# Two-layer hybrid encoder on one core: the second norm's sum moved into the middle of the second FFN pair, and three attention-projection tiles built together

## The chip, the cores and the metric

One core of a Trainium2 chip. A core has a matrix engine (TensorE, PE in the profile; its weight loads are listed apart as PEld), three engines for the rest (VectorE = DVE, ScalarE = ACT, GpSimd = POOL), and queues that issue transfers (SP = SyncE, and POOL). The metric is the device time of one execution in microseconds (us). Before the change it is 1625.27 us, the median of three runs (1622.42 to 1626.29).

## The reference

Two layers over 512 positions of 1024 channels. Each layer has three parallel branches (differential attention, a Conformer convolution, a Fourier mixing), which are gated, merged and projected, and then a SwiGLU FFN with its own RMSNorm. The change touches the attention branch's last projection and the FFN:

```python
gates = jax.nn.sigmoid(h @ w_gate[l] + b_gate[l]).reshape(b, s, N_BRANCH, d)
merged = gates[:, :, 0] * y_a + gates[:, :, 1] * y_b + gates[:, :, 2] * y_c   # y_a = att @ w_proj_a
x = x + merged @ w_out[l]

h2 = rmsnorm(x, norm2_g[l])
f_gate, f_up = jnp.split(h2 @ w_ffn_in[l], 2, axis=-1)
x = x + (jax.nn.silu(f_gate) * f_up) @ w_ffn_out[l]
```

`rmsnorm(x, g)` is `x * rsqrt(mean(x*x) + EPS) * g`, with one scale for each position. The hidden width of the FFN is 2816, which is 22 tiles of 128.

## The kernel before, in words

**Layout.** Activations lie transposed: a tile is 128 channels by 512 positions. Each operand of a matmul is split in a high part in a reduced format and a low part, the rest; a product is three matmuls (high x high, low x high, high x low). Weights come as chunks of 128x1024 by DMA and are split on chip: ScalarE casts the high part, and VectorE subtracts (L210, L317), or ScalarE negates and a transfer issued by POOL adds the weights on top (L309, L331).

**Order.** The kernel gives each instruction a priority, `self.t`, a running clock of TensorE work; `self.at(t)` sets it. A scheduler, which runs when the program is built, sorts the instructions of all engines by these priorities and by its own model of what is ready. Each engine then takes its own list strictly from the front. The lists differ from the code's order, so the sections below show rows of these lists.

**Attention projection.** `main` first builds the attention outputs `self.atts`, four pairs of tiles (high, low); the last one becomes ready last. `gemm_two` (L237) takes two output tiles m=0 and 1 and runs the first three of four steps for both, then the last step for both. `gemm` (L223) runs the other six tiles one by one.

**The FFN's first half.** After the output projection, `combine` makes the operands of Strassen's scheme with half-size blocks. `pair_gemm` (L370) computes gate and up of one hidden tile (a pair) with seven block products in two PSUM banks, `b1` and `b2`. Four of the products come first (`first`, 12 matmuls each: a11, s1, s3, s2, 48 matmuls of 128x256). Then `p15` keeps a sum of the two banks (a copy on ScalarE, L389, and an addition on VectorE, L390), and three more products (a12, s4, a22; 36 matmuls) go into the same banks. Pairs use the banks in turn: tag "s" for pair 0, "att" for pair 1, "main" for pair 2, and "s" again for pair 3. So the first matmul of pair 3 must wait until `unit` of pair 0 has read both "s" banks.

**The second norm.** The weights are applied to x before it is normalised, and the scale `rb2` is multiplied in afterwards, in `unit` (L605: L608 to L617). `sq_add` collects the squares of x as the output projection makes them (a square on ScalarE, L411, and an addition on POOL, L416). `inv_rms` (L419) adds them over channels with one matmul against a matrix of ones (tile `oth`, float32), then makes 1/sqrt by a table function on ScalarE (L428) and one Newton step: L426 and L431, L432 on VectorE, L430 on ScalarE. With its last argument `True` the ones matmul is ordered behind the last matmul issued so far (`self.after`). It is called after the whole of pair 1 (L633, L634), and the units of pairs 0 and 1 follow.

**Rounds.** Hidden tiles are taken in rounds of 6, 6, 6 and 4; after each round the round's part of the second FFN matrix is multiplied (L642). All 48 first matmuls of a pair need its split weights: tiles `whi`, `wlo`, and the sums s1, s2, s4 in `qst`/`kst` for even pairs, `A` for odd ones. Halves of the weights of odd pairs come into `cv` tiles; VectorE's first sum of a pair (L310) waits for these transfers.

Of the kernel before, what the change touches and what calls it, by code (L numbers as in the profile page):

```python
# [18 lines left out]
D = 1024  # L19
T = 512  # L20
NT = T // P
KT = D // P
# [35 lines left out]
LAG_N = 5000  # L58
LAG_S = 20000
LAST = (2500, 8000)  # L60
LN = (6000, 14000, 29000)
PEORD = False
CONV_LOW = -20000
# [30 lines left out]
class Hybrid:  # L94
# [139 lines left out]
        self.at(self.t)  # L234
        return ps

    def gemm_two(self, xs):  # L237
        banks = [self.bank(), self.bank()]
        n = len(xs)
        ws = [[self.wtile() for _ in xs] for _ in banks]  # L240
        for ks in (range(n - 1), (n - 1,)):
            for ps, w in zip(banks, ws):
                for k in ks:
                    wh, wl = w[k]
                    xh, xl = xs[k]
                    self.at(self.t)
                    self.mm(ps, wh, xh, k == 0, False)
                    self.mm(ps, wh, xl, False, False)
                    self.lastmm = self.mm(ps, wl, xh, False, k == n - 1)
                    self.t += 3 * PASS  # L250
                    self.poll()
        self.at(self.t)
        return banks
# [113 lines left out]
                out[n] = (hi[:, s], lo[:, s])  # L367
        return out

    def pair_gemm(self, u, w, xc, split_k=False):  # L370
        nc = self.nc
        tag = ("s", "att", "main")[u % 3]
        b1, b2 = self.bank(tag), self.bank(tag)
        h = T // 2
        n = len(xc)

        def x(name):
            return [p[name] for p in xc]

        first = (  # L380
            (b1[:, 0:h], "a11", "b11", True), (b1[:, h:T], "s1", "t1", False),
            (b2[:, h:T], "s3", "t3", True), (b2[:, 0:h], "s2", "t2", False),
        )
        steps = (list(range(n - 1)), [n - 1]) if split_k else (list(range(n)),)
        for ks in steps:
            for i, (ps, a, b, start) in enumerate(first):
                self.product(ps, w[a], x(b), ks, start and ks[0] == 0, i % 2 == 1 and ks[-1] == n - 1)
        p15 = self.slot("M")
        nc.scalar.copy(p15, b1)  # L389
        nc.vector.tensor_tensor(out=p15, in0=b2, in1=p15, op=ALU.add)  # L390
        ks = list(range(n))
        self.product(b1[:, 0:h], w["a12"], x("b21"), ks, False, False)
        self.product(b1[:, h:T], w["s4"], x("b22"), ks, False, True)
        self.product(b2[:, h:T], w["a22"], x("t4"), ks, False, True)
        return b1, b2, p15
# [153 lines left out]
    def main(self, l):  # L549
        nc = self.nc  # L550
        self.by_dma = False
        self.glu(l)
        if l == 0:
            self.tables()
        self.qkv(l)
        self.heads(l, self.t + ATT0, ATT)
        self.by_dma = True
        self.four_c(l)
        merged = self.merged
        ths = []  # L560
        for m in range(KT):
            pg = self.gemm(self.h)
            ths.append(self.tanh(pg, 0, m, "A"))
        thb = [self.tanh(self.gemm(self.h), 1, m, "M") for m in range(LEAD_B)]
        self.drain("conv")
        for m in range(KT):
            py = self.gemm(self.cvs)
            self.merge(m, thb.pop(0), py)
            if m + LEAD_B < KT:
                thb.append(self.tanh(self.gemm(self.h), 1, m + LEAD_B, "M"))  # L570
        self.drain("att")
        ms = []

        def merge_a(m, py):
            self.merge(m, ths[m], py)
            ms.append(self.split_to(merged[m], "cv" if m < 4 else "A"))

        for m, py in enumerate(self.gemm_two(self.atts)):
            merge_a(m, py)
        for m in range(2, KT):  # L580
            merge_a(m, self.gemm(self.atts))
        self.by_dma = False
        x2, xc, acc = [None] * KT, [], None
        g2 = self.par(l, "g2")
        h = T // 2
        for q in range(KT // 2):
            us = self.wtp.tile([P, 2, T], F32, tag="wth", name=self.nm("us"))
            ts = self.wtp.tile([P, 2, T], F32, tag="wtl", name=self.nm("ts"))
            for i, m in enumerate((q, q + KT // 2)):
                xr = self.slot("M")  # L590
                self.at(self.t - 20000)
                getattr(nc, QS[3]).dma_start(xr, self.xin[m])
                self.at(self.t)
                ps = self.gemm(ms)
                xt = self.slot("V")
                nc.vector.scalar_tensor_tensor(out=xt, in0=ps, scalar=0.5, in1=xr, op0=ALU.mult, op1=ALU.add)
                nc.scalar.activation(us[:, i, :], xt, AF.Copy, scale=g2[:, m : m + 1])
                acc = self.sq_add(xt, acc, "M")
                x2[m] = xt
            xc.append(self.combine(us[:, 0, :], us[:, 1, :], (ts[:, 0, :], ts[:, 1, :]), XCT[q]))  # L600
        self.xg, self.acc = [], None
        xin = []
        rb2 = None

        def unit(j, b1, b2, qw, scaled):  # L605
            z = self.slot("M")
            v = nc.vector.tensor_tensor
            v(out=z[:, 0:h], in0=b1[:, 0:h], in1=rb2[:, 0:h], op=ALU.mult)  # L608
            v(out=z[:, h:T], in0=b1[:, h:T], in1=qw[:, 0:h], op=ALU.add)
            v(out=z[:, h:T], in0=z[:, h:T], in1=rb2[:, h:T], op=ALU.mult)  # L610
            nc.scalar.activation(z, z, AF.Silu)
            u = self.slot("M")
            v(out=u[:, 0:h], in0=b2[:, h:T], in1=qw[:, 0:h], op=ALU.add)
            v(out=u[:, h:T], in0=qw[:, 0:h], in1=qw[:, h:T], op=ALU.add)
            if scaled:
                v(out=u, in0=u, in1=rb2, op=ALU.mult)
            v(out=u, in0=u, in1=z, op=ALU.mult)  # L617
            if j < 4:
                t = self.wtp.tile([P, 2, T], F32R, tag="wth" if j < 2 else "wtl", name=self.nm("act"))
                return self.split(u, t[:, 0, :], t[:, 1, :])  # L620
            return self.split_to(u, "att")

        done = 0
        for rnd, nj in enumerate(ROUNDS):
            act = []
            held = []
            scaled = done + nj == NJ
            for j in range(nj):
                w = self.pair_weights(done + j)
                held.append((j, *self.pair_gemm(done + j, w, xc, done + j == 0), scaled))  # L630
                if done + j == 0:
                    continue
                if done + j == 1:  # L633
                    rb2 = self.inv_rms(acc, D, "ar", "rb", True)  # L634
                while held:
                    act.append(unit(*held.pop(0)))
            done += nj
            for m in range(KT):
                if scaled and l == L - 1 and m == KT - 1:
                    self.last_tile(m, act, x2[m])  # L640
                    continue
                y = ps = self.gemm(act)  # L642
                if not scaled:
                    y = self.slot("M")
                    nc.vector.tensor_tensor(out=y, in0=ps, in1=rb2, op=ALU.mult)  # L645
                nc.vector.tensor_tensor(out=x2[m], in0=y, in1=x2[m], op=ALU.add)
                if done < NJ:
                    continue
                if l == L - 1:
                    nc.sync.dma_start(self.out[m], x2[m])  # L650
                else:
                    sc = self.dram.tile([P, T], F32, tag=f"x{l}_{m}", name=f"x{l}_{m}")
                    getattr(nc, QS[3]).dma_start(sc, x2[m])
                    xin.append(sc)
                    self.next_x(l + 1, m, x2[m])
        self.xin = xin
        self.x = x2
# [208 lines left out]
    def heads(self, l, t0, span):  # L866
# [45 lines left out]
        def norm(hp):  # L912
            fs[hp] = self.head_cols(atts[hp], zs.pop(hp))
            self.t += 860
# [5 lines left out]
        for u in range(NH * NT):  # L920
# [7 lines left out]
            if u % 8 == 7:  # L928
                dn, ds = (LAG_N, LAG_S) if u < NH * NT - 1 else LAST
                self.later(t + LAG_T + LAG_V + dn, "att", lambda hp=u // 8: norm(hp))  # L930
# [166 lines left out]
    def conv(self, l, t0, span):  # L1097
# [82 lines left out]
        def up(fn):  # L1180
            self.at(self.tc.cur_priority - LN_UP)
            fn()

        t1 = t0 + span + PAUSE[1]
        for fn, dt in zip((ln0, ln1, ln2), LN):
            self.later(t1 + dt, "conv", lambda fn=fn: up(fn))
# [136 lines left out]
```

## Time and profile before

| what | value |
|---|---|
| median of 3 runs | 1625.27 us (1622.42 to 1626.29) |
| profiled execution, its own time | 1623.3 us |
| its span, first to last instruction | 1621.5 us |
| TensorE busy | 1593.5 us, 98% of the span |
| VectorE, ScalarE, POOL busy | 1309.1, 870.6, 183.6 us |
| mean granted TensorE clock | 0.993 of full speed |

The time is that of the execution, and the span leaves out 1.8 us around the instructions. A matmul's busy time is modelled and overlaps that of the next, so the distance between the starts of two matmuls is the better measure: 0.12 us for a 128x256 matmul of the FFN pairs at full clock. A view of waits names for each engine what it sat idle for, and a view by time lists instructions with their start, duration, and in square brackets the idle time before them and what ended it.

### The profile page before, as it was taken

What the parts mean: (1) busy time and instruction counts of PE and PEld (TensorE: products, weight loads), DVE (VectorE), ACT (ScalarE), POOL (GpSimd) and SP (SyncE); (2) the same over time, 40 slices, a digit from 0 to 9 for tenths busy, and PEclk for the clock granted to TensorE, in tenths of its full rate; (3) what the DMA queues carried; (4) which work ended last, traced back from release to release, by engine and by line L of the source; (5) the groups of instructions that cost most, each with busy time, mean ns of one, the idle gap of its engine ahead of it and who ended that gap; (6) DMA issues with size and microseconds to landing.
All of it is one profiled execution on the core that took longest, in us unless ns stands there. A gap on an engine that the chain in (4) does not pass through costs nothing.

```text
span 1621.5 us, 24447 instructions
## 1 busy us (share of the span) xinstructions
PE 1593.5 (98%) x9104; PEld 1395.3 (86%) x9104; DVE 1309.1 (81%) x2388; ACT 870.6 (54%) x1419; POOL 183.6 (11%) x162
## 2 busy tenths in 40 slices
PE   9999999999998999999999999999999899999999
PEld 7888888787888898999888888887878898989998
DVE  6999999775887786858779999996758878878684
ACT  6546556873565463535444565577635644546351
POOL 1000010113230000000100000020232300000000
PEclk9999999999999999999999999999999999999999
DMA  6556366455463554647432664554445535546361
GB/s 220 169 165 197 83 163 150 112 127 124 150 168 79 156 131 124 150 111 186 127 117 80 196 180 118 137 147 111 119 116 162 144 92 151 136 130 157 87 161 65
DMA packets 80471, 222.85 MB, mean 137 GB/s; under 512 B 11216, under 2 KB 12368, under 8 KB 80352
## 3 DMA queue, kind: packets, MB, share of 16 engines
q1 hardware_dynamic: 67392, 175.59, 34.5%
q0 software_dynamic: 12528, 45.17, 16.2%
q8 instruction: 72, 1.18, 0.3%
q10 hardware_dynamic: 432, 0.53, 0.1%
q14 instruction: 47, 0.39, 0.1%
HBM read 207.35 MB, written 13.89 MB: 136 GB/s over the span
## 4 chain that ended last, share of the span: by engine, by line
PE 92%; DVE 3%; DMA 2%; ACT 1%; issue 1%; SPq 0%; DVEq 0%; ACTq 0%
PE main L126 54%; PE s L342 10%; PE att L342 8%; PE main L342 8%; PE s L126 4%; PE att L126 3%; PE oth L126 3%; PE att L136 2%; DMA cv<-in_w 1%; DMA wr<-in_w 0%; PE att L835 0%; DVE wl L210 0%; DVE A L160 0%; DMA V<-in_xT 0%; DMA kst<-dqk 0%
## 5 line engine op out<-in xcount | busy, mean ns | idle before, releaser
L208 ACT CAST wh<-wr 128x1024 fp32r<-128x1024 f32 x178 | 186.2, 1050 | 244.2 <-PE main L126 130.5
L126 PE MATMUL main<-X,wh 128*128 128x512 f32 x864 | 278.6, 395 | 0.0
L210 DVE TENSOR_TENSOR wl<-wr,wh 128x1024 fp32r<-128x1024 f32 x138 | 176.6, 1280 | 37.6 <-ACT wh L208 37.0
L126 PEld LDWEIGHTS main<-X,wh 128*128 128x128 f32 x864 | 161.0, 189 | 32.5 <-issue 0.3
L1120 DVE SCALAR_TENSOR_TENSOR cv<-cv,hcw,cv 128x497 f32<-128x497 f32 (+14 forms) x240 | 180.4, 752 | 0.9
L126 PE MATMUL main<-X,wl 128*128 128x512 f32 x432 | 169.9, 393 | 0.0
L126 PE MATMUL main<-act,wh 128*128 128x512 f32 (+1 forms) x520 | 161.9, 391 | 0.0
L944 ACT ACTIVATE at<-s,mx 128x512 f32<-128x512 f32 x128 | 87.9, 688 | 59.0 <-DVE mx L942 50.2
L126 PEld LDWEIGHTS main<-act,wh 128*128 128x128 f32 x520 | 96.3, 188 | 21.7 <-DVE M L645 0.6
L126 PE MATMUL main<-A,wh 128*128 128x512 f32 x320 | 107.7, 393 | 0.0
L309 POOL DMA_DIRECT2D wlo<-in_w x44 | 37.8, 859 | 577.7 <-ACT wlo L308 172.9
L126 PE MATMUL main<-att,wh 128*128 128x512 f32 x320 | 100.0, 393 | 3.0 <-ACT att L159 3.0
L942 DVE TENSOR_REDUCE mx<-s 128x1 f32<-128x512 f32 x128 | 86.6, 683 | 19.3 <-PE s L126 18.7
L126 PE MATMUL main<-act,wl 128*128 128x512 f32 (+1 forms) x260 | 101.4, 391 | 0.0
L126 PE MATMUL main<-wh,X 128*128 128x512 f32 x288 | 96.7, 392 | 0.0
L126 PEld LDWEIGHTS main<-X,wl 128*128 128x128 f32 x432 | 81.5, 189 | 16.5
L331 POOL DMA_DIRECT2D wl<-in_w x40 | 34.5, 864 | 518.9 <-ACT wl L330 357.2
L126 PE MATMUL main<-cv,wh 128*128 128x512 f32 x240 | 76.8, 392 | 0.0
L126 PEld LDWEIGHTS main<-att,wh 128*128 128x128 f32 x320 | 59.7, 188 | 17.4 <-ACT att L159 3.5
L126 PE MATMUL main<-A,wl 128*128 128x512 f32 x192 | 74.4, 390 | 0.0
L126 PEld LDWEIGHTS main<-A,wh 128*128 128x128 f32 x320 | 59.7, 188 | 11.9
L126 PEld LDWEIGHTS main<-wh,X 128*128 128x128 f32 x288 | 53.8, 188 | 11.1
(371 smaller groups left out, 4206.7 us busy)
## 6 DMA issues: line engine op xcount, KB each, us to landing
wr<-in_w SPq DMA_DIRECT2D x222, 512.0 KB, 3.8
wlo<-in_w POOLq DMA_DIRECT2D x44, 512.0 KB, 5.6
wl<-in_w POOLq DMA_DIRECT2D x40, 512.0 KB, 7.6
cv<-in_w SPq DMA_DIRECT2D x80, 256.0 KB, 4.7
dqk<-at SPq DMA_DIRECT2D x32, 256.0 KB, 4.6
qst<-dqk SPq DMA_DIRECT2D x96, 64.0 KB, 2.2
kst<-dqk SPq DMA_DIRECT2D x96, 64.0 KB, 2.0
V<-in_xT SPq DMA_DIRECT2D x8, 256.0 KB, 7.1
```

Source lines behind the costliest of these rows:

```text
L126: return self.pin(self.nc.tensor.matmul(out, lhsT=lhsT, rhs=rhs, start=start, stop=stop))
L136: self.pin(self.nc.tensor.transpose(ps[:, s], src[:, s], self.ident))
L208: nc.scalar.copy(hi, raw)
L210: nc.vector.tensor_tensor(out=lo, in0=raw, in1=hi.bitcast(F32), op=ALU.subtract)
L309: nc.gpsimd.dma_start(l2, src2, accum_op=ALU.add)
L331: self.nc.gpsimd.dma_start(lo, src, accum_op=ALU.add)
L342: self.nc.tensor.matmul(ps, lhsT=a[:, s], rhs=b, start=start and k == ks[0] and i == 0, stop=last and i == 2, skip_group_check=True,)
L942: nc.vector.tensor_reduce(out=mx, in_=ps, axis=AX.X, op=ALU.max, negate=True)
L944: nc.scalar.activation(e, ps, AF.Exp, bias=mx, accum_out=z1 if c else z0)
L1120: ins = nc.vector.scalar_tensor_tensor(out=acc[:, a:b], in0=g[:, a + d : b + d], scalar=w[:, t : t + 1], in1=acc[:, a:b], op0=ALU.mult, op ...
```

## The change

Two parts.

1. `gemm_two` becomes `gemm_few(xs, few)` and is called with 3: three attention-projection tiles run their first three steps, and then their last.
2. `pair_gemm` gets an argument `mid`, a function that it calls between the four first products and the `p15` copy. For pair 1 that function is `norm`, which calls `inv_rms` with a priority 15000 earlier than the running clock. So the ones matmul is tied to the last matmul of pair 1's first four products, where it was tied to the last matmul of the pair, and all instructions of `inv_rms` get an earlier priority.

```diff
+EARLY = 15000
...
-    def gemm_two(self, xs):
-        banks = [self.bank(), self.bank()]
+    def gemm_few(self, xs, few):
+        banks = [self.bank() for _ in range(few)]
...
-    def pair_gemm(self, u, w, xc, split_k=False):
+    def pair_gemm(self, u, w, xc, split_k=False, mid=None):
...
                 self.product(ps, w[a], x(b), ks, start and ks[0] == 0, i % 2 == 1 and ks[-1] == n - 1)
+        if mid is not None:
+            mid()
         p15 = self.slot("M")
...
-        for m, py in enumerate(self.gemm_two(self.atts)):
+        for m, py in enumerate(self.gemm_few(self.atts, 3)):
             merge_a(m, py)
-        for m in range(2, KT):
+        for m in range(3, KT):
             merge_a(m, self.gemm(self.atts))
...
+        def norm():
+            nonlocal rb2
+            self.at(self.t - EARLY)
+            rb2 = self.inv_rms(acc, D, "ar", "rb", True)
+            self.at(self.t)
+
...
-                held.append((j, *self.pair_gemm(done + j, w, xc, done + j == 0), scaled))
+                held.append((j, *self.pair_gemm(done + j, w, xc, done + j == 0, norm if done + j == 1 else None), scaled))
                 if done + j == 0:
                     continue
-                if done + j == 1:
-                    rb2 = self.inv_rms(acc, D, "ar", "rb", True)
                 while held:
```

No instruction is added or removed. Line numbers below 60 stay, later ones grow by 1 to 9 (L342 becomes L343, L426 becomes L429, L608 becomes L617). How the lists of the engines change is shown at three places, all in the first layer; the second layer has the same moves.

**TensorE in the FFN's first round, before.** `att` are the banks of pair 1, `main` those of pair 2, `oth` the ones matmul.

```order
L342 MATMUL att_4883<-B_4719,whi_4855 128x256
L342 MATMUL att_4883<-B_4720,whi_4855 128x256
L342 MATMUL att_4883<-B_4719,wlo_4856 128x256
L126 MATMUL oth_4971<-M_4701,ones 128x512
L342 MATMUL main_5036<-at_4411,whi_5011 128x256 x2
```

The same engine with the change; `s` are the banks of pair 0.

```order
L343 MATMUL att_4883<-B_4715,A_4871 128x256
L343 MATMUL att_4883<-B_4716,A_4871 128x256
L343 MATMUL att_4883<-B_4715,A_4872 128x256
L127 MATMUL oth_4932<-M_4701,ones 128x512
L343 MATMUL s_4754<-X_4414,whi_4731 128x256
```

The ones matmul stood behind the last product of pair 1; it now stands behind pair 1's first four products and ahead of the last three of both pair 0 and pair 1, 72 matmuls earlier.

**VectorE in the same stretch, before.** `ar` and `rb` are the norm's tiles; `cv_5281` and `cv_5418` are first sums of the weights of pairs 4 and 5; `s_4754` is bank `b1` of pair 0, read by its unit.

```order
L426 TENSOR_SCALAR ar_4973<-oth_4971 128x512
L310 TENSOR_TENSOR cv_5418<-cv_5410,cv_5414 128x512
L431 SCALAR_TENSOR_TENSOR ar_4973<-ar_4977,ar_4973 128x512
L160 TENSOR_TENSOR kst_5294<-cv_5281,qst_5293 128x512
L311 TENSOR_TENSOR cv_5410<-cv_5412,cv_5410 128x512
L432 SCALAR_TENSOR_TENSOR rb_4975<-ar_4973,rb_4975 128x512
L160 TENSOR_TENSOR A_5433<-cv_5418,A_5432 128x512
L321 TENSOR_TENSOR cv_5281<-wr_5279,cv_5282 128x512
L312 TENSOR_TENSOR cv_5419<-cv_5414,cv_5410 128x512
L608 TENSOR_TENSOR M_4981<-s_4754,rb_4975 128x256
L609 TENSOR_TENSOR M_4981<-s_4754,M_4804 128x256
```

VectorE with the change:

```order
L318 TENSOR_TENSOR wlo_5012<-wr_5005,whi_5011 128x1024
L429 TENSOR_SCALAR ar_4934<-oth_4932 128x512
L161 TENSOR_TENSOR kst_5027<-cv_5010,qst_5026 128x512
L161 TENSOR_TENSOR A_5173<-cv_5145,A_5172 128x512
L161 TENSOR_TENSOR kst_5033<-cv_5009,qst_5032 128x512
L434 SCALAR_TENSOR_TENSOR ar_4934<-ar_4938,ar_4934 128x512
L435 SCALAR_TENSOR_TENSOR rb_4936<-ar_4934,rb_4936 128x512
L311 TENSOR_TENSOR cv_5281<-wr_5277,wr_5279 128x512
L617 TENSOR_TENSOR M_4981<-s_4754,rb_4936 128x256
L618 TENSOR_TENSOR M_4981<-s_4754,M_4804 128x256
L622 TENSOR_TENSOR M_4986<-s_4755,M_4804 128x256
```

The norm's three instructions and pair 0's unit stood behind the first sums of both pair 4 (`cv_5281`) and pair 5 (`cv_5418`). The norm now stands ahead of both, and the unit's readers of the "s" banks behind that of pair 4 alone.

**TensorE in the attention projection, before.** `main_4150`, `main_4151` and `main_4194` are output tiles 0, 1 and 2; `att_3949` is the last attention output, and the transposes `oth_3943` lead to it.

```order
L126 MATMUL main_4194<-att_3679,wl_4198 128x512
L136 MATMUL oth_3943<-ident,at_3863 128x128 x4
L126 MATMUL main_4150<-att_3949,wh_4154 128x512
L126 MATMUL main_4151<-att_3949,wh_4154 128x512
L126 MATMUL main_4194<-att_3949,wh_4197 128x512
```

With the change:

```order
L127 MATMUL main_4152<-att_3679,wl_4162 128x512
L137 MATMUL oth_3943<-ident,at_3863 128x128 x4
L127 MATMUL main_4150<-att_3949,wh_4155 128x512
L127 MATMUL main_4151<-att_3949,wh_4155 128x512
L127 MATMUL main_4152<-att_3949,wh_4161 128x512
```

Nothing moves here: the scheduler had already put the first three steps of tile 2 ahead of the transposes, and only the names of tiles differ.

## The prediction

> **What bounds the kernel now.** I read the busy shares first, then the chain of work that ended last, and then who waited for whom on the engine that carries the chain.
>
> ```profile
> span 1621.5 us, 24447 instructions
> ...
> PE 1593.5 (98%) x9104; PEld 1395.3 (86%) x9104; DVE 1309.1 (81%) x2388; ACT 870.6 (54%) x1419; POOL 183.6 (11%) x162
> ...
> PE 92%; DVE 3%; DMA 2%; ACT 1%; issue 1%; SPq 0%; DVEq 0%; ACTq 0%
> ...
> PE s L342 <- DVE M L609: 8.8, 2, 4.4
> PE s L126 <- DMA kst<-dqk: 3.8, 1, 3.8
> PE main L126 <- ACT att L159: 3.0, 2, 1.5
> ```
>
> TensorE is the bound: 98% busy, 92% of the chain. A change can gain only where TensorE sits idle or runs slowly. The last three rows (engine and line, what it waited for; us in total, times, longest) are its largest waits. The first is the FFN's pair 3, which needs the "s" banks that pair 0's unit still holds, once per layer. The third is the attention projection's last step. Those two are what the change speaks of. The second lies in layer 1's attention, behind transfers of what TensorE itself computed, so it moves along with TensorE.
>
> Next, TensorE by time around the first wait, in both layers.
>
> ```profile
> 471.42 0.63 PE L342 MATMUL s<-X,whi 128*128 128x256 f32 x2
> ...
> 480.37 1.02 PE L126 MATMUL oth<-M,ones 128*128 128x512 f32 x2
> ...
> 481.59 0.40 PE L342 MATMUL main<-at,whi 128*128 128x256 f32 x2
> ...
> 486.62 0.40 PE L342 MATMUL main<-B,qst 128*128 128x256 f32 x2
> 486.86 0.28 PE L342 MATMUL main<-B,kst 128*128 128x256 f32 x1
> ...
> 491.54 0.77 PE L342 MATMUL s<-at,whi 128*128 128x256 f32 x2 [4.40 <-DVE M L609]
> ...
> 496.47 0.40 PE L342 MATMUL s<-X,whi 128*128 128x256 f32 x2
> ...
> 1278.43 0.40 PE L342 MATMUL s<-X,whi 128*128 128x256 f32 x2
> ...
> 1293.55 0.28 PE L342 MATMUL main<-B,kst 128*128 128x256 f32 x1
> ...
> 1298.25 0.77 PE L342 MATMUL s<-at,whi 128*128 128x256 f32 x2 [4.43 <-DVE M L609]
> ...
> 1302.68 0.40 PE L342 MATMUL s<-X,whi 128*128 128x256 f32 x2
> ```
>
> Two matmuls of 486.62 take 0.24 us to the next start, so one takes 0.12 us. The next would have started at 486.98 in layer 0 and at 1293.67 in layer 1. It started 4.56 and 4.58 us later.
>
> The stall has a tail, which the table by stretches shows (TensorE, its loads, VectorE, ScalarE, POOL busy; granted clock; DMA share; GB/s):
>
> ```profile
> 487.20:491.50 4.30, 0.00 (x0) 0.00 (x0) 4.30 (x9) 2.38 (x3) 0.86 (x1) 0.74 0.24 15
> 491.50:496.50 5.00, 4.96 (x25) 4.99 (x26) 3.88 (x9) 1.92 (x2) 0.00 (x0) 0.54 0.47 92
> 496.50:531.00 34.50, 34.50 (x279) 33.98 (x278) 23.44 (x43) 16.02 (x27) 0.87 (x1) 1.00 0.34 92
> ...
> 1298.20:1303.20 5.00, 4.95 (x29) 4.98 (x30) 4.02 (x10) 2.56 (x4) 0.00 (x0) 0.66 0.48 91
> ```
>
> After the pause the granted clock is 0.54 and 0.66 for some 5 us, then full to the round's end, where TensorE is busy without a gap (34.50 of 34.50).
>
> **Why pair 3 waits.** VectorE and ScalarE in that stretch:
>
> ```profile
> 472.44 1.21 DVE L317 TENSOR_TENSOR wlo<-wr,whi 128x1024 fp32r<-128x1024 f32 x1
> ...
> 475.35 0.69 DVE L160 TENSOR_TENSOR kst<-cv,qst 128x512 fp32r<-128x512 f32 x1 [0.50 <-ACT qst L159]
> ...
> 479.29 0.69 DVE L310 TENSOR_TENSOR cv<-wr,wr 128x512 f32<-128x512 f32 x1 [3.25 <-DMA wr<-in_w]
> ...
> 481.35 1.29 DVE L317 TENSOR_TENSOR wlo<-cv,whi 128x512 fp32r<-128x512 f32 x2
> 482.56 0.68 DVE L426 TENSOR_SCALAR ar<-oth 128x512 f32<-128x512 f32 x1
> ...
> 485.82 0.69 DVE L310 TENSOR_TENSOR cv<-cv,cv 128x512 f32<-128x512 f32 x1 [2.58 <-DMA cv<-in_w]
> ...
> 488.24 0.68 DVE L432 SCALAR_TENSOR_TENSOR rb<-ar,rb 128x512 f32<-128x512 f32 x1
> ...
> 490.65 0.42 DVE L608 TENSOR_TENSOR M<-s,rb 128x256 f32<-128x256 f32 x1
> 490.98 0.41 DVE L609 TENSOR_TENSOR M<-s,M 128x256 f32<-128x256 f32 x1
> ...
> 473.18 0.63 ACT L159 CAST A<-cv 128x512 fp32r<-128x512 f32 x1
> ...
> 481.62 1.28 ACT L428 ACT_TABLE_LOAD   x1
> 483.28 0.69 ACT L428 ACTIVATE rb<-oth,eps 128x512 f32<-128x512 f32 x1 [0.38 <-DVE ar L426]
> 484.00 0.63 ACT L430 ACTIVATE ar<-rb 128x512 f32<-128x512 f32 x1
> ...
> 499.07 0.57 ACT L389 COPY M<-main 128x512 f32<-128x512 f32 x1
> ```
>
> The ones matmul (480.37) comes late, and in VectorE's list the two later steps of the norm stand behind `L310` of pair 5, which sits 2.58 us for a transfer. Three more weight instructions stand between `L432` and pair 0's unit. Only `L609` frees bank b1, and TensorE starts at 491.54.
>
> **The change part by part.**
>
> *Ones matmul, moved by 72 matmuls.* From 480.37 to 481.59 it and three 0.12 us matmuls take 1.22 us, so it costs 0.86 us. It costs that at either place: net 0. At the new place the clock is just recovering from the short stalls before 467 (start distances of 0.21 us at 471.42). If the whole 0.86 us ran at half clock it would cost another 0.9 us per layer; but the slow spell lasts some time, not some number of matmuls, so other work escapes it. I take 0.
>
> *Norm and unit 0, moved ahead.* I replay VectorE from rows. The ones matmul starts at 471.42 and is modelled at 1.02 us: its result is there by 472.5. `L429` follows the 1.21 us `wlo` and runs from 473.6 to 474.2. ScalarE finishes its cast of 473.18 at 473.7; the table load takes 1.28, to 475.0, the root 0.69, to 475.7; then comes the `qst` cast and the square, to 476.9. Before, VectorE's `kst` began at 475.35; it waits for that cast and ends near 476.9. The two norm steps end near 478.1. `L311` of pair 4 waits for its transfer until 479.29, as before, and ends at 479.9 (start distances of such instructions are 0.6). `L617` and `L618` take 0.33 each: the bank is free at 480.6. TensorE, whose work up to there is the same, asks at 486.98. Cover: 6.4 us. The stall goes, with its slow clock: 4.56 + 4.58 = 9.14 us of waiting.
>
> *The slow clock.* From 491.54 to 496.47 there are 24 matmuls, 4.93 us where 24 x 0.12 = 2.88; excess 2.05. From 1298.25 to 1302.68 it is 4.43 - 2.88 = 1.55. Together 3.60 us.
>
> [...]
>
> *What is late next.* The weights of pair 3 now stand behind the unit. Its `wlo` (before at 481.35) now follows, from 479.9 on, seven short instructions of units 0 and 1 (0.33 each) and one of 0.6, and its two halves of 0.6 end near 484; TensorE asks at about 487.2. Cover 3 us. After pair 3's 48 matmuls (5.76 us) TensorE goes on, near 492.8, to pair 2's last products, which need the copy `L392` of `main` (before at 499.07). On ScalarE it stands behind the second table load, two `L620`, four casts, a 1.05 us cast and a negation; I get 489.6, cover 3. Neither is thin enough to cost anything; if one were 5 us late, its layer would lose 2 us and perhaps the slow clock again.
>
> *Projection.* Its wait is 1.5 us per layer, and TensorE's list shows that three tiles shared it already. Bounds: a gain of 3.0 us if the waiting vanished, nothing if the list decides. Identical lists give identical waits: 0.
>
> Sum: 9.14 + 3.60 = 12.74 us. The rest of the program is driven by TensorE and moves forward as a block. The span of 1621.5 us becomes 1608.8, and with the 1.8 us around it the profiled execution of 1623.3 us becomes 1610.6. It lies 2.0 below the median of the runs shown, so the median goes from 1625.27 to **1612.5 us**, 0.78% less.
>
> **Rivals.**
>
> 1. *Forecast*: both stalls and their slow clocks go. 1612.5; own range 1609 to 1616. Chance 0.76.
>
> 2. *Half of it*: the pause is replaced by a shorter one at pair 3's `wlo` or at pair 2's copy, 3 us late in each layer. Gain 12.74 - 6 = 6.7, so 1618.6. For it: the norm's table load and the unit now stand ahead of weight work on two lists that run strictly in order. Against it: the covers of 3 us above. Chance 0.11.
>
> 3. *It changes nothing*: the bank waits for the transfer that `L311` still needs, and not for the norm. That transfer landed 6.4 us ahead of need in layer 0; in layer 1 the row is
>
> ```profile
> 1286.83 0.69 DVE L310 TENSOR_TENSOR cv<-wr,wr 128x512 f32<-128x512 f32 x1 [4.10 <-DMA wr<-in_w]
> ```
>
> which with 0.60 + 0.66 frees the bank at 1288.1, 5.6 ahead of 1293.67. It must land 6 to 11 us later to bring the stall back. Time 1625. Chance 0.08.
>
> 4. *Slower*: TensorE itself now waits for POOL. The ones matmul reads the sum of squares, and behind it the whole list stands. The last additions:
>
> ```profile
> 456.64 1.47 POOL L416 TENSOR_TENSOR M<-M,M 128x512 f32<-128x512 f32 x1 [0.46 <-DVE cv L312]
> ...
> 463.41 6.15 POOL L416 TENSOR_TENSOR M<-M,M 128x512 f32<-128x512 f32 x1 [5.31 <-ACT M L411]
> ...
> 1270.21 6.15 POOL L416 TENSOR_TENSOR M<-M,M 128x512 f32<-128x512 f32 x1 [5.31 <-ACT M L411]
> ```
>
> The last one takes 6.15 us where its neighbour takes 1.47, and ends at 469.56 and 1276.36. TensorE arrives at 471.42 and 1278.43: a cover of 1.9 and 2.1 us, where it had 10.8 before. The loss begins with an addition longer than 8.0 us, and exceeds the gain (6.4 per layer) beyond 8.0 + 6.4 = 14.4 us; at three times 6.15 it is 18.45 - 8.0 = 10.4 per layer, so 1625.3 - 12.7 + 20.9 = 1633. Against it: nothing ahead of this place changes, and both layers show 6.15. Chance 0.05.
>
> [...]
>
> **How the numbers follow.** Differences under 0.3% (4.9 us) can't be told from none here; "faster" means below 1620.4. Rivals 1 and 2 lie below it (0.87, of which I leave 0.01 for noise), rival 3 within, rival 4 above. So faster 0.86, same 0.10, slower 0.04, as a small POOL wait would still end within. The range is 1608.5 to 1618.7: below, the projection's 3.0 us and a run at the lower edge of the spread; above, rival 2. Rivals 3 and 4 are left out.
>
> **What would show it.** Right: the wait of `s` for VectorE is gone from TensorE's list of waits, the clock is 1.00 where pair 3 starts, the ones matmul starts near 471.4 without a wait for POOL, and `L618` runs near 480.3. The attention wait stays at 1.5 us twice. Wrong: a new row of TensorE waiting for POOL `M`, for VectorE `wlo` or for ScalarE `M`, or pair 3 that starts no earlier. The end of the program should come 12 to 13 us earlier, half of it within the first layer.

## The result and the profile after

The changed kernel takes **1607.84 us** (median of 4 runs, 1605.44 to 1608.71), beside 1625.15 us (1622.42 to 1626.29) for the kernel before on the same chip. The ratio is 0.9894 with a 95% interval of 0.9876 to 0.9911: a gain of 17.3 us, between 14.5 and 20.2. The prediction was 1612.5 us, a gain of 12.7. The direction was right and the time lies 0.7 us below the range.

From the page of the changed kernel: the span, the busy times, and the chain of work that ended last.

```profile
span 1603.7 us, 24440 instructions
...
PE 1585.8 (99%) x9104; PEld 1387.5 (87%) x9104; DVE 1307.9 (82%) x2388; ACT 869.9 (54%) x1419; POOL 183.5 (11%) x162
...
PE 95%; DVE 2%; DMA 1%; ACT 1%; issue 0%; SPq 0%; ACTq 0%
```

The count of all instructions falls by 7, but the four engines have as many as before. TensorE's share of the chain rose from 92% to 95%. Its waits (us in total, times, longest):

```profile
PE s L127 <- DMA kst<-dqk: 3.0, 1, 3.0
PE main L127 <- ACT att L160: 3.0, 2, 1.5
PE s L343 <- ACT B L160: 1.5, 2, 0.7
PE att L343 <- DVE wlo L318: 1.3, 2, 0.7
PE s L343 <- DVE B L161: 1.3, 2, 0.7
```

The row of 8.8 us for the "s" banks is gone, and no row took its place. The projection's 3.0 us stand as before. The last three rows are short stalls of some 0.7 us ahead of the changed place; they were there before too (1.5, 1.5 and 1.3 us), and they matter below.

TensorE in the first layer, by time (start, duration, instruction): the ones matmul, the first matmul of pair 3, and pair 2's last products.

```profile
469.22 1.02 PE L127 MATMUL oth<-M,ones 128*128 128x512 f32 x2
...
484.47 0.40 PE L343 MATMUL s<-at,whi 128*128 128x256 f32 x2
...
490.23 0.40 PE L343 MATMUL main<-X,whi 128*128 128x256 f32 x2
```

None has a bracket: none waited. VectorE in the same stretch:

```profile
472.55 0.68 DVE L429 TENSOR_SCALAR ar<-oth 128x512 f32<-128x512 f32 x1
...
476.65 0.69 DVE L435 SCALAR_TENSOR_TENSOR rb<-ar,rb 128x512 f32<-128x512 f32 x1
478.01 0.69 DVE L311 TENSOR_TENSOR cv<-wr,wr 128x512 f32<-128x512 f32 x1 [0.67 <-DMA wr<-in_w]
...
478.95 0.42 DVE L618 TENSOR_TENSOR M<-s,M 128x256 f32<-128x256 f32 x1
...
481.55 1.29 DVE L318 TENSOR_TENSOR wlo<-cv,whi 128x512 fp32r<-128x512 f32 x2
482.75 0.69 DVE L313 TENSOR_TENSOR cv<-wr,wr 128x512 f32<-128x512 f32 x1
```

`L618`, which frees the bank, runs at 478.95 where it ran at 490.98. The next instruction follows it by 0.34 us, so the bank is free at 479.3, 5.2 us ahead of TensorE.

**Where the 17.8 us of the profiled executions are.** The spans are 1621.5 and 1603.7. Matmuls of one kind and place can be set side by side. As fixed points I use, in each layer, the last short stall of the FFN's first round (`s<-B,qst`) and one matmul of `main` some 63 us later. In the first layer they are, before the change,

```profile
467.27 0.39 PE L342 MATMUL s<-B,qst 128*128 128x256 f32 x1 [0.65 <-DVE B L160]
...
530.08 0.28 PE L342 MATMUL main<-X,wlo 128*128 128x256 f32 x1
```

and after it

```profile
466.24 0.39 PE L343 MATMUL s<-B,qst 128*128 128x256 f32 x1 [0.66 <-DVE B L161]
...
520.97 0.28 PE L343 MATMUL main<-X,wlo 128*128 128x256 f32 x1
```

This stretch took 62.81 us and takes 54.73: 8.08 less. In the second layer it is 61.98 and 54.48: 7.50 less. Up to the first fixed point the changed kernel is 1.03 us ahead, and between the two layers it gains 1.23, 0.8 of them at a wait for transfers of `kst` (3.8 and 3.0 us). The change touches neither place. Of the 1.03 us, 0.96 arise in the program's first 19 us, at waits for the first split weights and in a granted clock of 0.58 there before (8 to 12 us). The point itself lies at 466.3 to 468.8 us in the six profiles with the old order in the first layer and at 466.2 to 467.3 in the six with the new one; the wait for transfers in layer 1's attention is 2.4 to 3.8 us in the profiles, in either order. So 15.58 us lie where the change is, and 2.3 elsewhere, where nothing ties them to the change.

The prediction had 6.61 and 6.13 us for the two stretches. The missing 1.5 and 1.4 us are not in the pause. They lie ahead of it: from the last short stall to the moment at which TensorE asks for the "s" banks it was 19.71 us (467.27 to 486.98) and is 18.23 (466.24 to 484.47), and in the second layer 19.60 and 18.22. The table by stretches of the kernel before, with TensorE, its loads, VectorE, ScalarE and POOL busy, then the granted clock, DMA share and GB/s:

```profile
468.00:472.00 4.00, 4.00 (x23) 4.00 (x23) 4.00 (x6) 3.98 (x7) 1.56 (x1) 0.59 0.00 0
1274.00:1278.00 4.00, 3.93 (x20) 3.93 (x21) 4.00 (x6) 3.48 (x6) 2.36 (x1) 0.57 0.02 6
```

The same place, right behind the short stalls, with the change:

```profile
468.00:472.00 4.00, 4.00 (x31) 3.52 (x30) 4.00 (x6) 4.00 (x6) 1.38 (x2) 1.00 0.00 0
1264.00:1268.00 4.00, 4.00 (x29) 3.45 (x29) 4.00 (x6) 3.85 (x6) 2.05 (x1) 1.00 0.02 6
```

Before, the granted clock behind the short stalls was 0.59 and 0.57 in the mean of these 4 us. After, it stayed full in both layers. This is ahead of everything that the change moves, except the ones matmul. Whether the change did it or chance, and what such a drop costs in either kernel, is what the experiments had to settle.

### The profile page after: what moved, and what is told of

It is laid out like the page before. It is cut to its first block, busy times and chain, and to the rows that moved or that the text cites. A ratio compares the mean times of both kernels' runs of the same rounds, so it can differ in the third digit from the quotient of the medians.

```text
span 1603.7 us, 24440 instructions
## 1 busy us (share of the span) xinstructions
PE 1585.8 (99%) x9104; PEld 1387.5 (87%) x9104; DVE 1307.9 (82%) x2388; ACT 869.9 (54%) x1419; POOL 183.5 (11%) x162
## 3 DMA queue, kind: packets, MB, share of 16 engines
q0 software_dynamic: 12528, 45.17, 16.2%
## 4 chain that ended last, share of the span: by engine, by line
PE 95%; DVE 2%; DMA 1%; ACT 1%; issue 0%; SPq 0%; ACTq 0%
PE main L127 57%; PE s L343 9%; PE main L343 9%; PE att L343 8%; PE s L127 4%; PE att L127 3%; PE oth L127 3%; PE att L137 2%; DMA wraw<-in_w 0%; PE att L842 0%; DVE A L161 0%; DMA kst<-dqk 0%; SPq L866 0%; DMA wr<-in_w 0%; PE oth L137 0%
```

## The experiments

Theory A: the change is worth what the prediction's sum says, plus whatever chance adds. Theory B: in the kernel before, the end of the pause belongs to VectorE and a transfer and not to TensorE, so time that TensorE loses ahead of the pause costs nothing there, while in the changed kernel it costs its full length. Theory C: the change itself keeps the clock up behind the short stalls. The medians and ratios:

| run | what runs | median, us | ratio to before, 95% interval |
|---|---|---|---|
| e1_norm_only | tie and due time, no third tile | 1606.96 | 0.9893 [0.9877, 0.9910] |
| e2_three_only | third tile alone | 1624.09 | 0.9994 [0.9985, 1.0003] |
| e5_early_only | due time and third tile, no tie | 1624.16 | 1.0006 [0.9995, 1.0017] |
| e4_tie_only | tie and third tile, due time as before | 1607.73 | 0.9892 [0.9876, 0.9909] |
| e9_layer0 | whole change, first layer only | 1615.50 | 0.9943 [0.9928, 0.9958] |
| e12_layer1 | whole change, second layer only | 1616.09 | 0.9952 [0.9934, 0.9969] |
| e8_fill | before, 38 idle matmuls in each pause | 1622.43 | 0.9986 [0.9977, 0.9996] |
| e10_fill58 | before, 58 idle matmuls in each pause | 1621.72 | 0.9990 [0.9980, 0.9999] |
| e7_tie_pair0 | sum tied to pair 0 instead of pair 1 | 1610.29 | 0.9914 [0.9899, 0.9929] |
| e6_four_tiles | the change, with four tiles behind one wait | 1608.08 | 0.9898 [0.9883, 0.9913] |

The kernel before took 1624.97 us beside e1, e2, e8 and e9, 1623.92 beside e4, e6, e7 and e10, and 1623.35 beside e5 and e12.

### Which part of the change does it

```diff
 # e1_norm_only, against the changed kernel
-        for m, py in enumerate(self.gemm_few(self.atts, 3)):
+        for m, py in enumerate(self.gemm_few(self.atts, 2)):
...
-        for m in range(3, KT):
+        for m in range(2, KT):
 # e2_three_only, against the changed kernel: the sum asked for behind the whole of pair 1, EARLY = 0
-EARLY = 15000
+EARLY = 0
...
-                held.append((j, *self.pair_gemm(done + j, w, xc, done + j == 0, norm if done + j == 1 else None), scaled))
+                held.append((j, *self.pair_gemm(done + j, w, xc, done + j == 0), scaled))
...
+                if done + j == 1:
+                    norm()
 # e5_early_only: as e2_three_only, with EARLY = 15000
 # e4_tie_only, against the changed kernel
-EARLY = 15000
+EARLY = 0
```

> Only the norm's move; the projection is as before (two tiles). All engines' lists are those of the whole change, row for row. Theory A (all of the gain is the norm's move): the time of the whole change, 1605 to 1609 us, 17 us under the kernel before. Theory B (the three projection tiles carry the 4.6 us that the prediction missed): about 1612.5. For the slow clock after the short stalls near 467 and 1274 us (1.3 and 1.6 us in the profile before, none in the profile of the whole change): if it is chance, this profile may show it in either layer and the time then moves by 1.5 us for each; if the move itself removes it, it shows in neither.

> Only the three projection tiles; the norm is tied as before. Theory A: the time of the kernel before, 1622 to 1626 us, with the wait of 1.5 us in the projection and the two pauses of 4.4 us still there. Theory B: 4 to 5 us faster than before. The profile also shows a second time whether the slow clock near 467 and 1274 us belongs to the kernel before (theory: tied to the kernel) or comes and goes (theory: chance).

> The vector work's earlier due time (EARLY 15000) without the tie: the norm's sum is asked for at the end of the second pair, as before, with three projection tiles. Its lists on the engines are those of the kernel before, so theory 'only the tie does anything' expects before's time within 0.15% and the wait of s for DVE M of 4.4 to 7 us in each layer, the longer where the clock stays full behind the short stalls. Rival 'putting the scale first on VectorE gives part of the gain': 4 us or more below before.

> The tie to the middle of pair 1 alone: two projection tiles as before and the vector work's due time not moved. Its lists of instructions on the engines are those of the whole change, so theory 'only the tie does anything' expects the changed kernel's time, 1607 to 1608, and a stretch from the last short stall to the mark 63 us later in before of 54.6 us where the clock stays full, and of about 56.2 us where it drops after the short stalls. Rival 'the early vector work is worth something of its own': 2 us or more above that.

(The text on e4 says two projection tiles; the kernel that ran has three. Between two and three nothing moves in the engines' lists.)

e1 and e4 take the time of the whole change, e2 and e5 that of the kernel before. So the tie to the middle of pair 1 is the change. The third tile and the earlier due time are worth nothing: with the tie, the lists are the same with or without them, and without the tie they are those of the kernel before. The two kernels that run before's order add something else. TensorE's waits of e2,

```profile
PE s L343 <- DVE M L618: 11.6, 2, 7.0
```

and of e5:

```profile
PE s L343 <- DVE M L618: 13.5, 2, 6.8
```

The two pauses amount to 11.6 and 13.5 us here, and to 8.8 in the prediction's profile, at the same time of the whole. Where the pause is long, the clock did not drop ahead of it. In e5, both layers, behind the short stalls:

```profile
468.00:472.00 4.00, 4.00 (x36) 4.00 (x35) 4.00 (x6) 4.00 (x6) 1.38 (x2) 1.00 0.00 0
...
1274.00:1278.00 4.00, 4.00 (x36) 4.00 (x35) 4.00 (x6) 4.00 (x6) 0.90 (x2) 1.00 0.00 0
```

And the pause ends no earlier. TensorE in e5, by time:

```profile
466.32 0.39 PE L343 MATMUL s<-B,qst 128*128 128x256 f32 x1 [0.66 <-DVE B L161]
...
484.43 0.28 PE L343 MATMUL main<-B,kst 128*128 128x256 f32 x1
...
491.42 0.55 PE L343 MATMUL s<-at,whi 128*128 128x256 f32 x1 [6.71 <-DVE M L618]
```

The two executions stand 0.95 us apart at the last short stall, so I count from there. TensorE ran out of work 18.23 us behind it (484.43 + 0.12 - 466.32), 1.5 us earlier than in the prediction's profile (19.71), and went on after 25.10, where that one has 24.27 (491.54 - 467.27). What ends the pause is on VectorE:

```profile
485.70 0.69 DVE L311 TENSOR_TENSOR cv<-cv,cv 128x512 f32<-128x512 f32 x1 [3.66 <-DMA cv<-in_w]
490.53 0.42 DVE L617 TENSOR_TENSOR M<-s,rb 128x256 f32<-128x256 f32 x1
```

From the landing of pair 5's transfer to `L617` it is 4.83 us here, 4.82 in e2, and 490.65 - 485.82 = 4.83 in the kernel before: a fixed string of VectorE work behind a transfer. Counted as above, the transfer landed after 19.38 us here and after 18.55 there. The second layer shows the same: 4.82 and 4.83 us of VectorE work, behind a landing at 19.43 and 18.46. So theory B holds: the 1.5 us by which TensorE is earlier are not passed on, and time that it loses ahead of the pause is taken out of the pause. That the transfer even lands 0.8 to 1.0 us later when TensorE is earlier was not explained.

### One layer at a time

```diff
 # e9_layer0, against the changed kernel; e12_layer1 has the two conditions exchanged
-                held.append((j, *self.pair_gemm(done + j, w, xc, done + j == 0, norm if done + j == 1 else None), scaled))
+                held.append((j, *self.pair_gemm(done + j, w, xc, done + j == 0, norm if done + j == 1 and l == 0 else None), scaled))
...
+                if done + j == 1 and l > 0:
+                    norm()
```

> The change in the first layer only; in the second the norm is tied as before. If each layer's pause and its slow clock are worth what the trace shows (6.6 and 6.1 us): 1625.2 - 6.6 = 1618.5 and up to 1.5 more by the slow clock of the short stall in layer 0, so 1617 to 1618.5. If the missing 4.6 us belong to the whole program, about half of 17.3 is won: 1616.5. The pause of 4.4 us stays in the second layer alone.

> The change in the second layer alone, the first layer as before. From the last short stall to the mark 62.8 us later, the second layer took 62.0 us as before and 54.5 us changed, the first 62.8 to 64.3 as before and 54.7 to 56.2 changed. If the two layers don't influence each other, the time is 7.5 us below before, about 1616.5, and this and the change in the first layer alone (9.1 to 9.5 us) add up to the whole (16 to 18 us). By the prediction's replay it would be 6.13 us, 1618. The first layer should show a wait of s for DVE M of 4.4 us with, and of about 7 us without a slow clock right behind the short stalls.

The first layer alone is worth 9.5 us (1624.97 - 1615.50, interval 6.8 to 11.7), 0.8 more than the larger of the two gains that the text on e9 expected. The second is worth 7.3 (1623.35 - 1616.09), as expected, and its unchanged first layer shows the long wait, 6.6 us, at full clock. Together they are 16.7: they add up to the whole. Each profile holds one layer of either order, and here the clock did drop behind the short stalls in changed layers. The first layer of e9:

```profile
468.00:472.00 4.00, 4.00 (x21) 3.76 (x20) 3.90 (x6) 3.98 (x8) 1.37 (x2) 0.57 0.00 0
```

the second layer of e12:

```profile
1278.00:1282.00 4.00, 4.00 (x22) 3.86 (x22) 4.00 (x6) 4.00 (x7) 1.61 (x1) 0.62 0.01 2
```

and the first layer of e4:

```profile
468.00:472.00 4.00, 4.00 (x22) 3.52 (x22) 3.92 (x6) 4.00 (x6) 1.37 (x2) 0.72 0.00 0
```

So theory C falls: the change does not prevent the drop. All profiles, with the stretch between the two fixed points, in us; "dropped" gives the clock found in the 3 or 4 us behind the short stalls:

| order in that layer | first layer: clock, pause, stretch | second layer: clock, pause, stretch |
|---|---|---|
| as before: before | dropped 0.59, 4.40, 62.81 | dropped 0.57, 4.43, 61.98 |
| as before: e2 | full, 7.04, 64.31 | dropped 0.70, 4.54, 62.03 |
| as before: e5 | full, 6.71, 63.64 | full, 6.77, 63.48 |
| as before: e12, e9 | full, 6.57, 63.98 (e12) | dropped 0.65, 3.97, 61.55 (e9) |
| changed: after | full, none, 54.73 | full, none, 54.48 |
| changed: e1 | full, none, 54.71 | full, none, 54.48 |
| changed: e4 | dropped 0.72, none, 56.20 | full, none, 54.48 |
| changed: e6 | full, none, 54.76 | full, none, 54.49 |
| changed: e9, e12 | dropped 0.57, none, 56.23 (e9) | dropped 0.62, none, 55.86 (e12) |

The drop comes in 4 of 8 layers of the old order and in 3 of 10 of the new. In the new order it costs 1.5 us in the first layer (56.2 against 54.7) and 1.4 in the second (55.86 against 54.48). In the old order it costs nothing; the stretches with it are even the shorter ones, by 1.2 us in the first layer and 1.6 in the second. The drop is free there because the end of the pause does not hang on TensorE. Of the 1.2 and 1.6 us, 0.9 and 1.1 are a pause that ends earlier, counted from the last short stall (24.27 us against 24.96 to 25.42 in the first layer, 23.74 to 24.29 against 25.15 in the second). The rest is a shorter slow spell behind it (in the first layer some 4.5 us of it in the kernel before and in e5, and 5.5 in e12; in the second 3.35 in the kernel before and 4.6 in e5).

When the drop comes can be read from the traces. The first layer of the kernel before, in three stretches behind the last short stall:

```profile
468.60:468.74 0.14, 0.14 (x4) 0.14 (x3) 0.14 (x1) 0.14 (x1) 0.14 (x1) 1.00 0.00 0
468.74:472.15 3.41, 3.41 (x18) 3.41 (x18) 3.41 (x5) 3.41 (x6) 0.82 (x1) 0.50 0.00 0
472.16:472.30 0.14, 0.14 (x3) 0.14 (x3) 0.14 (x1) 0.14 (x2) 0.11 (x1) 1.00 0.00 0
```

Here the clock is halved from 468.74 to 472.15. In the traces a slow spell lasts 3.41 us or a multiple of that at 0.50 (in this one 3.41 us five times, with 8 to 18 matmuls in it, and 6.83 us once; the program's end cuts the last one off). All changes of the clock within one execution lie on one grid of 3.41 us (in this one at 7.94, 11.36, 468.74, 472.16, 489.22, 496.05 us and on, in the changed kernel's at 1113.49, 1116.91 and 1605.01), which stands differently to the program from execution to execution. Counted from the start of the matmul that ends the last short stall, the next point of this grid lay 0.22 to 1.47 us later in the seven layers with a drop, and the drop began there. In the eleven without one it lay at 0.02 or at 1.52 to 3.36. The last two short stalls are 1.4 us of idle time within 1.9 us, so the drop came where both lay clearly inside the 3.41 us between two points. Nothing ties the position of the grid to the change, and the stretch of 1.3 us in 3.41 makes an estimate of four layers in ten with a drop, in either order. So what theory A calls chance is whether the clock drops, and theory B is why that counts only in the changed kernel. No run moved the grid, and idle time alone is no full rule: in e6 a single stall of 1.70 us between two points was not followed by a drop, and in e8 one of 1.74 was.

### The slow clock behind the pause

```diff
 # against the kernel before; FILL = 38 in e8_fill, 58 in e10_fill58
+FILL = 38
...
+        if u == 2:
+            self.fill(xc[0]["b11"][0])
         p15 = self.slot("M")
...
+    def fill(self, x):
+        ps = self.bank("oth")
+        for _ in range(FILL):
+            self.after(self.mm(ps[:, 0 : T // 2], x[:, 0:P], x, True, True))
```

The added matmuls are of 128x256, go into a spare bank, and nobody reads them; they only keep TensorE at work in the pause.

> The kernel before with 38 matmuls of 128x256 added in each layer between the last product of pair 2 and the first of pair 3, on a bank that nobody reads; they fill the pause (38 x 0.12 = 4.56 us). If the pause is set by VectorE and the slow clock behind it by TensorE's idleness: pair 3 starts as late as before, the granted clock stays at 1.00 behind it, and 3.6 us are won (1621.5 against 1625.2). If the slow clock has another cause: no gain, same time as before. If the pause is not VectorE's: 9 us lost.

> The kernel before with 58 instead of 38 idle matmuls of 0.12 us in each pause (6.96 us, as much as the longest pause seen, 7.04 us), so that TensorE doesn't stand still at all. If the slow clock behind the pause is paid for by the standing still (2.05 us in the first layer, 1.55 us in the second), the granted clock stays 1.00 behind the pause and the time is 3.6 us below before, about 1621.4. Theory 'the end of the pause belongs to VectorE' adds: the first product behind the pause starts no earlier than in before, 24 to 25.5 us behind the last short stall, and nothing of the pause itself comes back. Rival 'the pause is TensorE's own': the filler delays what ends it, and the time rises by up to 14 us.

With 38 of them TensorE still waited 2.35 and 2.64 us. The clock behind that did not stay at 1.00, as the text on e8 expected; it was 0.66 over the next 5 us in both layers, and the time fell by only 0.14% (interval 0.04 to 0.23%). With 58 the pause was covered but for 0.46 us in the first layer, and the clock stayed full behind it. The table by stretches of e10, where the prediction's profile had 0.54:

```profile
491.50:496.50 5.00, 4.54 (x38) 4.34 (x37) 4.05 (x12) 2.03 (x3) 0.00 (x0) 1.00 0.64 108
```

The time fell by 2.2 us (0.2 to 3.2), and not by 3.6. TensorE's waits in e10 show why:

```profile
PE main L343 <- ACT M L392: 1.7, 2, 1.2
```

At full clock TensorE reaches pair 2's last products before ScalarE's copy of `main` is done, and waits 1.2 and 0.6 us. In the kernel before, the copy ended at 499.64 and TensorE came to these products at 499.82, at the slow clock, so part of that clock's price was hidden behind ScalarE. And none of the pause itself came back: the first product behind the filler started at 492.24, 25.8 us behind the last short stall (24.3 to 25.4 in the first layers of that order without filler). Keeping TensorE busy did not move this pause, which a transfer and VectorE end.

### How early the sum may come

```diff
 # e7_tie_pair0, against the changed kernel
-                held.append((j, *self.pair_gemm(done + j, w, xc, done + j == 0, norm if done + j == 1 else None), scaled))
+                held.append((j, *self.pair_gemm(done + j, w, xc, done + j == 0, norm if done + j == 0 else None), scaled))
```

> The changed kernel with the sum tied to the first pair's middle, 14 matmuls (1.7 us) earlier. In the profile of the changed kernel POOL's last addition ends at 468.54 us and the ones-matmul starts at 469.22 us, so the cover is 0.68 us. If that cover is what the place decides, TensorE now waits for POOL about 1 us in each layer (a row of PE behind POOL M in the waits) and the time is about 2 us above the changed kernel, about 1610, and more if the clock drops behind it. If the addition is done earlier whenever it is asked for earlier, there is no such wait and the time is the changed kernel's, 1607 to 1608.

This is the prediction's rival 4, brought about by moving the ones matmul 14 matmuls further ahead. POOL's last addition, in the changed kernel,

```profile
462.38 6.16 POOL L419 TENSOR_TENSOR M<-M,M 128x512 f32<-128x512 f32 x1 [5.30 <-ACT M L414]
```

ends at 468.54, and the ones matmul started at 469.22: a cover of 0.68 us, where the prediction had 1.9, because the clock had dropped in its profile and TensorE came later. In e7 the cover is gone. TensorE by time:

```profile
469.23 2.07 PE L127 MATMUL oth<-M,ones 128*128 128x512 f32 x2 [0.87 <-POOL M L419]
```

and the clock behind this fourth stall:

```profile
468.00:472.00 4.00, 3.13 (x11) 1.89 (x10) 4.00 (x6) 4.00 (x7) 1.36 (x2) 0.62 0.00 0
...
1268.00:1272.00 4.00, 4.00 (x19) 3.09 (x18) 3.60 (x7) 3.24 (x5) 0.87 (x1) 0.61 0.15 14
```

The stretches are 57.33 and 57.22 us, 2.6 and 2.7 more than in the changed kernel at full clock, for waits of 0.9 us and the drops behind them. The median is only 2.6 us above e4, which ran beside it; in e4's own profile the clock dropped in one layer, and how often it does so in the other executions is not on record. The mechanism of rival 4 is real, and the kernel as changed stands less than 1 us from it.

### The projection's wait

```diff
 # e6_four_tiles, against the changed kernel
-    def gemm_few(self, xs, few):
-        banks = [self.bank() for _ in range(few)]
+    def gemm_few(self, xs, tags):
+        banks = [self.bank(tag) for tag in tags]
...
-        for m, py in enumerate(self.gemm_few(self.atts, 3)):
+        for m, py in enumerate(self.gemm_few(self.atts, ("main", "main", "main", "s"))):
```

> The changed kernel with four instead of three projection tiles behind one wait, the fourth in a bank of the s pair. The changed kernel still waits 1.49 us twice for ScalarE's last att tile. If the wait is short of work in front of it, the fourth tile's nine ready products (9 x 0.24 us = 2.2 us) cover it and the time falls by 3.0 us to about 1605. Rival: the work ahead of the last tile was there already with two and three, the wait stays 1.5 us twice, and the time stays 1607 to 1608. Rival on the other side: the s bank isn't free yet, and TensorE waits for it longer than 1.5 us.

The time is that of the changed kernel. TensorE's waits in e6:

```profile
PE att L343 <- DVE wlo L318: 3.0, 2, 1.7
...
PE main L127 <- ACT att L160: 1.0, 1, 1.0
PE main L127 <- DVE A L695: 0.9, 2, 0.5
...
PE main L127 <- DVE A L161: 0.7, 2, 0.4
```

A fourth tile does take 2.0 us from the projection's wait, but 1.6 us come back as longer waits in the FFN's first round (`wlo`) and two small new rows of 0.9 and 0.7. These rows wait for VectorE, which seems to be late by itself; that was not taken apart.

## Why the prediction was right and wrong

**The bound and the direction: right.** TensorE's pause at the "s" banks went, and its slow clock with it (the granted clock was 1.00 from 484.5 to 494.5 us and from 1278 to 1293); rivals 2 and 3 did not come about.

**The ones matmul and the norm: right in kind, earlier than replayed.** The ones matmul started at 469.22 (replayed 471.4), `L618` at 478.95 (480.3), pair 3's `wlo` was done at 482.75 (484), the copy `L392` ran at 487.80 (489.6). All are 1.2 to 2.2 us earlier. 1.03 us of that the changed kernel was already ahead at the last short stall; for the ones matmul the rest, 1.2 us, is the dropped clock of the prediction's profile (4.15 us behind that stall there, 2.98 here). The cover at the bank is 5.2 us (6.4 in the replay). The net price of 0 for the ones matmul stands: the stretch with a dropped clock, 56.20 us, is as long as the replay makes it (62.81 - 6.61), and the slow spells of 3.41 us in the kernel before hold 18, 16, 17 and 15 matmuls (from 468.74, 1124.10, 1274.29 and 1298.18 us), so it is their time that stays the same.

**The projection: right.** 0 us, with 3.0 us of waiting left.

**The step that failed: the size of the pause, 9.14 us, and the sentence that TensorE's work up to there "is the same" and asks at 486.98.** Both come from one execution in which the clock had dropped ahead of the pause in both layers. The replay kept these two drops in the changed kernel; it even quotes a start distance of 0.21 us right behind them. In the changed kernel's profile the clock held, and TensorE asked at 484.47: 1.48 us earlier in its stretch, and 1.38 in the second layer. For the case with drops the sum is right to 0.1 us. With the clock dropped in both layers, the stretches of the table give 62.81 - 56.2 = 6.6 and 61.85 - 55.86 = 6.0 us (61.85 is the mean of three), and the prediction had 6.61 and 6.13. With the clock full in both, they give 63.98 - 54.73 = 9.2 and 63.48 - 54.48 = 9.0, together 18.2. The kernel before takes the same time either way or a little longer when the clock holds (63.64 to 64.31 us in the first layer, against 62.81), because the pause takes up the difference; the changed kernel has no pause to take it up. With drops as often as in the table (half of the layers before, three in ten after) the gain of the two stretches is an estimate of 16.0 us, 3.3 more than forecast. The medians show 17.3 (14.5 to 20.2), 18.0 (e1) and 16.2 (e4).

**The step from the execution to the median: not settled.** The profiled execution lay 2.0 us below the median of before, and the prediction carried these 2 us over into the changed kernel. There the profiled execution lay 2.4 us below its median, so the step did no harm, but that is luck: nothing says why either lay low. The two drops are no explanation for before. The stretches with drops are 2.8 us shorter than those without, yet e5, without a drop, took 1622.46 us in its profiled execution, less than the 1623.3 with two.

**The slow clock, 3.60 us: too large as a term by itself, harmless in the sum.** Alone it is worth 2.2 us (0.2 to 3.2); waits of 1.2 and 0.6 us for ScalarE's copy stood behind it. Where the pause goes, that copy is early enough (`L392` at 487.80, asked for at 490.23), and the whole counts.

**Rival 4: it did not come about, but its cover was put too high.** The prediction had 1.9 and 2.1 us. It is 0.68 and 0.66 at full clock, and 0.9 us of waiting there cost 2.6 with the drop behind it (e7). Why POOL's last addition takes 6.15 us where the one ahead of it takes 1.47 is not shown by any run.

**Why the clock had dropped in that profile.** The same stalls of 0.65 to 0.74 us were followed by a drop in 7 of 18 layers, by where the grid of 3.41 us stood; only 1.4 us of idle time stand in the 3.41 us ahead of these drops.

**Open.** How much idle time between two points of the grid it takes for a drop, and on what the transfer hangs that ends the old pause. A filler in the short stalls themselves was not tried. Of executions without a trace only the time and the mean clock are on record. Among those of the kernel before beside e1, the ones at a mean clock of 0.996 took 1621.05 and 1622.49 us and those at 0.991 took 1626.09 and 1626.73, which suggests that a slow clock costs time somewhere else; where it lay in them is not known.

## What to carry to other kernels

Here a wait whose end another engine set swallowed what the waiting engine lost ahead of it: in e5 TensorE came to the pause 1.5 us earlier than in the prediction's profile (18.23 us behind the last short stall, against 19.71), and the pause ended no earlier (25.10 against 24.27). With the wait removed, those losses became visible (56.2 us with the drop, 54.7 without), and their absence became gain. So, before summing a pause, look at the clock in the stretch ahead of it, replay it at full clock as well, and read a second execution. And when a sum is tied earlier, read its cover at the earliest moment at which the engine can arrive, not at the one that one profile shows.

## What the runs showed of the hardware that was not expected

- Two stalls of TensorE of only 0.65 to 0.74 us within 1.9 us were followed by 3.41 us at half clock in 7 of 18 layers, namely where the next point of the grid on which the clock changes lay 0.22 to 1.47 us behind the start of the matmul that ends the second (0.02 or 1.52 to 3.36 us in the other eleven). The price was 1.4 to 1.5 us where nothing hid it. With a stall of 0.87 us more behind them (e7) the clock dropped in both layers of the profile (0.62 and 0.61 over 4 us).
- Kept at work through a pause of 7 us, TensorE kept its clock at 1.00 (e10, 491.5 to 496.5 us), where it was at 0.54 after standing still; and yet the gain was only 2.2 us of 1624: TensorE then waited 1.2 and 0.6 us for ScalarE.
